# A decoder block on one core: the down projection's first 24 chunks by Strassen's seven products, and the second norm's factor moved to up's input

## The chip, the cores and the metric

The kernel runs on one core of a Trainium2 chip. TensorE multiplies matrices, VectorE (DVE in rows), ScalarE (ACT) and GpSimd (POOL) work elementwise, SyncE (SP) issues most transfers between memory and the on-chip buffers, and 16 DMA engines carry them out. The metric is the device time of one execution in microseconds; less is better.

## The reference

All tensors are float32; 512 tokens of width 1024.

```python
h = rms_norm(x, norm_mix)
q, k, v, u = split(h @ w_in)
a = moba_attention(q, k, v)                 # 8 heads x 64, causal, ALiBi
p = multiscale_pool(u, w_pool, pool_scale)  # 4 groups x 128
x = x + concat(a, p) @ w_out
h = rms_norm(x, norm_mlp)
x = x + square(relu(h @ w_up)) @ w_down     # w_up: 1024 x 4096, w_down: 4096 x 1024
out = rms_norm(x, norm_final)
```

## The kernel before

A float32 product is three matmuls (`mm3`): each operand is split into hi (the value rounded to float32r, a cast on ScalarE) and lo (the rest, a subtraction on VectorE), and hi x hi, hi x lo and lo x hi are summed in a bank of the accumulator. Every engine issues its instructions in the order in which the program is written (`in_program_order`), so an instruction that waits holds up all that stand behind it on its engine.

Weights come in chunks of 512 KB (128 partitions x 1024 numbers). `load` takes the next chunk from the list `chunks` and loads it into one of three buffers `raw` through SyncE's queue. `next_split` splits the oldest loaded chunk into `whi` and `wlo` (four buffers each) and calls `load` again; the load waits until the split has read its buffer. `prefetch` puts split chunks on the list `ready`.

The second half of the block is what matters here. `out_tile` adds the output projection to a tile of 128 tokens; `gained` multiplies the tile by the norm's weights, `turn2` transposes and splits it, and `factor` computes the second norm's factor of each row, which is not needed until the end: since it is positive, its square may be applied where the rows of the down projection are added to x (`residual`, with `rr`). Up takes 32 chunks of 128 hidden features; for each, 24 matmuls make a bank of 128 features x 512 tokens, and `sqrelu` writes the squared relu to `r[f]`. The down projection takes the 32 chunks of `w_down` in order. For chunk f, `r_split` splits `r[f]`, and 24 matmuls (4 token tiles x 2 halves of the columns x 3) add to all eight banks, which hold the sums of the whole stage. The last four chunks are held back and applied tile by tile, so that the residual, the final norm and the store of one tile run beside the products of the next.

## Time and profile before

| | |
|---|---|
| three runs | 546.05, 546.06 and 546.46 us, median 546.06 |
| the profiled execution | span 546.4 us from its first to its last instruction; no other time of its own is given |
| TensorE busy | 98% of the span |
| VectorE, ScalarE, GpSimd busy | 51%, 39%, 10% |
| memory read | 49.55 MB, 95 GB/s over the span with what is written |

The profile is of one execution. A matmul's busy time overlaps that of the next, so TensorE's pace is read from the starts of its instructions, not from their durations. Idle time of an engine is given with what released it. Where a helper writes an instruction, its line is the helper's: L112 is the cast and L113 the subtraction of every split, L161 to L163 are the three matmuls of `mm3`.

### The profile page before, as it was taken

To read this page: it belongs to the slowest core of one execution; us is meant where nothing else is said; L and a number is where in the kernel's file an instruction comes from. 1 tells how busy PE (TensorE), PEld (TensorE's weight loads), DVE (VectorE), ACT (ScalarE), POOL (GpSimd) and SP (SyncE) were. 2 spreads that over 40 slices of the span, in tenths; PEclk is the share of its full clock that TensorE was granted. 3 is DMA by queue.
4 is the path that set the end of the run, shared out by engine and by line. 5 is a ranking of instruction groups with operands and counts; after the bars stand their busy time and mean duration, and the time that the engine had idled before them with its cause. 6 is when DMAs were issued, how large, how long until landed. Compare 5 with 4: busy or idle time off the path is not lost.

```text
span 546.4 us, 6441 instructions
## 1 busy us (share of the span) xinstructions
PE 533.8 (98%) x2495; PEld 445.6 (82%) x2495; DVE 277.6 (51%) x468; ACT 215.4 (39%) x385; POOL 53.8 (10%) x55
## 2 busy tenths in 40 slices
...
GB/s 287 137 115 40 64 129 10 122 12 110 80 114 148 7 40 128 143 93 100 95 99 100 93 100 93 115 78 115 77 116 77 116 79 114 80 113 115 2 38 115
DMA packets 55904, 52.06 MB, mean 95 GB/s; under 512 B 2241, under 2 KB 47809, under 8 KB 55874
## 3 DMA queue, kind: packets, MB, share of 16 engines
...
q10 hardware_dynamic: 578, 1.05, 0.5%
...
HBM read 49.55 MB, written 2.10 MB: 95 GB/s over the span
## 4 chain that ended last, share of the span: by engine, by line
PE 89%; DVE 5%; ACT 2%; issue 2%; DMA 1%; SPq 0%; POOL 0%; POOLq 0%
PE bank L162 27%; PE bank L161 27%; PE bank L163 27%; PE bank L261 4%; PE bank L394 2%; DMA wvr<-in_w_in_dram 1%; PE bank L183 1%; PE bank L423 1%; DVE ptl L429 1%; DVE p L400 1%; DVE wlo L113 1%; DVE ka L366 1%; DVE mx L476 0%; PE bank L441 0%; DVE mx L475 0%
## 5 line engine op out<-in xcount | busy, mean ns | idle before, releaser
L161 PE MATMUL bank<-hh,whi 128*128 128x512 f32 (+1 forms) x376 | 141.7, 377 | 0.2 <-DVE qs L356 0.2
L163 PE MATMUL bank<-hh,wlo 128*128 128x512 f32 (+1 forms) x376 | 141.3, 376 | 0.0
L162 PE MATMUL bank<-hl,whi 128*128 128x512 f32 (+1 forms) x376 | 141.2, 376 | 0.0
L113 DVE TENSOR_TENSOR wlo<-raw,whi 128x1024 fp32r<-128x1024 f32 x73 | 90.4, 1242 | 97.6 <-ACT whi L112 97.3
L112 ACT CAST whi<-raw 128x1024 fp32r<-128x1024 f32 x76 | 79.5, 1055 | 92.7 <-PE bank L163 92.3
L161 PE MATMUL bank<-whi,rh 128*128 128x512 f32 x224 | 87.1, 389 | 0.0
L162 PE MATMUL bank<-wlo,rh 128*128 128x512 f32 x224 | 87.1, 389 | 0.0
L163 PE MATMUL bank<-whi,rl 128*128 128x512 f32 x224 | 87.1, 389 | 0.0
L161 PEld LDWEIGHTS bank<-hh,whi 128*128 128x128 f32 x376 | 70.8, 188 | 13.3 <-PE bank L423 0.4
L162 PEld LDWEIGHTS bank<-hl,whi 128*128 128x128 f32 x376 | 70.8, 188 | 12.8
L163 PEld LDWEIGHTS bank<-hh,wlo 128*128 128x128 f32 x376 | 70.8, 188 | 12.7
L630 DVE TENSOR_TENSOR r<-bank,z 128x512 f32<-128x512 f32 (+1 forms) x35 | 22.6, 645 | 97.2 <-ACT z L629 97.2
L629 ACT ACTIVATE z<-bank 128x512 f32<-128x512 f32 (+1 forms) x35 | 19.7, 562 | 118.1 <-PE bank L163 118.1
L161 PEld LDWEIGHTS bank<-whi,rh 128*128 128x128 f32 x224 | 42.1, 188 | 8.8
L163 PEld LDWEIGHTS bank<-whi,rl 128*128 128x128 f32 x224 | 42.1, 188 | 8.7
L162 PEld LDWEIGHTS bank<-wlo,rh 128*128 128x128 f32 x224 | 42.1, 188 | 8.6
L176 POOL TENSOR_TENSOR rstd<-ms,mhalf 128x1 f32<-128x1 f32 x8 | 4.4, 556 | 408.9 <-DVE ms L171 408.9
L113 DVE TENSOR_TENSOR rl<-r,rh 128x512 fp32r<-128x512 f32 x32 | 21.8, 684 | 4.7 <-ACT rh L112 4.7
L402 ACT ACTIVATE p<-p,mn 128x128 f32<-128x128 f32 (+3 forms) x32 | 18.0, 561 | 11.5 <-DVE rs L381 5.8
L112 ACT CAST rh<-r 128x512 fp32r<-128x512 f32 x32 | 19.8, 619 | 5.4 <-PE bank L162 5.4
L167 ACT ACTIVATE sq<-x 128x512 f32<-128x512 f32 (+2 forms) x17 | 10.3, 610 | 17.2 <-DVE x L658 17.2
L382 DVE TENSOR_SCALAR p<-p,rs 128x128 f32<-128x128 f32 (+3 forms) x32 | 16.0, 501 | 1.1
...
## 6 DMA issues: line engine op xcount, KB each, us to landing
raw<-in_w_up_dram SPq DMA_DIRECT2D x32, 512.0 KB, 4.0
raw<-in_w_down_dram SPq DMA_DIRECT2D x32, 512.0 KB, 3.3
raw<-in_w_in_dram SPq DMA_DIRECT2D x12, 512.0 KB, 4.1
raw<-in_w_out_dram SPq DMA_DIRECT2D x8, 512.0 KB, 3.3
wvr<-in_w_in_dram SPq DMA_DIRECT2D x4, 512.0 KB, 8.6
x<-in_x_dram SPq DMA_DIRECT2D x3, 512.0 KB, 9.7
out_dram<-o SPq DMA_DIRECT2D x4, 256.0 KB, 2.0
out_dram<-o ACTq DMA_DIRECT2D x4, 256.0 KB, 2.5
```

The source lines that it names most:

```text
L112: nc.scalar.copy(hi, src)
L113: (sub or nc.vector).tensor_sub(lo, src, as32(hi))
L161: nc.tensor.matmul(acc, lhsT=a[0], rhs=b[0], start=first, stop=False)
L162: nc.tensor.matmul(acc, lhsT=a[0], rhs=b[1], start=False, stop=False)
L163: nc.tensor.matmul(acc, lhsT=a[1], rhs=b[0], start=False, stop=last)
L167: nc.scalar.activation(dump, src, AF.Square, scale=1.0 / 32, accum_out=ss[:, k:k + 1])
L261: nc.tensor.matmul(acc, lhsT=a, rhs=w, start=n == 0 and kd == 0, stop=n == 2 and kd == KD - 1)
L382: nc.vector.tensor_scalar_mul(p[:, :w], p[:, :w], rs)
L394: nc.tensor.matmul(by_qi[qi], lhsT=qs[:, tok(qi)], rhs=k[:, :w], start=n == 0, stop=n == 1)
L402: nc.scalar.activation(p[:, :w], p[:, :w], AF.Exp, scale=-1.0, bias=mn, accum_out=sm)
L629: nc.scalar.activation(z[:, sl], acc, AF.Relu)
L630: nc.vector.tensor_mul(r[f][:, sl], acc, z[:, sl])
```

## The change

The first 24 chunks of the down projection are taken in 12 pairs. In a pair, the left operand is a 2 x 2 matrix of blocks (two chunks of features x two halves of the tokens) and so are the weights (two chunks x two halves of the columns). The four blocks of their product are made from seven products of sums of blocks in place of eight products. The eight banks can't hold seven products of two banks each, so there are two sweeps over the pairs: the first sums four products (m1, m6, m7, m4), whose banks are then read out into x and a helper tile y; the second sums three (m5, m2, m3). The sums of the token blocks are made on VectorE while up runs (`a_sums`, into `a_p`), and split once for each sweep (`a_split`). Of the four sums of weight blocks two are made on VectorE (`b_sums`) and two by a second DMA that GpSimd issues and that adds to what SyncE's load has put into the buffer (`accum_op`). Each chunk is loaded once for each sweep, whole or by half. A fourth `raw` buffer is added. The last eight chunks stay as they were, four as a plain loop and four tile by tile.

Because Strassen's sums mix token tiles, the second norm's factor can no longer be applied at the end: `normed2` applies it to up's input, after the squares (`squares`, `mean_of`, and `rsqrt`, a power on GpSimd); `gained`, `factor` and `rr` are gone, and `residual` is a plain addition.

```diff
 RAW = 3
+PAIRS = 12
...
     chunks += [cols_of(w_up_v, f * P) for f in range(NF)]
-    chunks += [rows_of(w_down, f) for f in range(NF)]
-    raws = []
+    for sweep in range(2):
+        for f in range(2 * PAIRS):
+            chunks.append(rows_of(w_down, f) + ((sweep, f % 2, f),))
+    chunks += [rows_of(w_down, f) for f in range(2 * PAIRS, NF)]
+    raws, more = [], []
     def load():
         if chunks:
-            src, shape = chunks.pop(0)
-            raw = wp.tile([P] + shape, F32, tag="raw", name="raw", bufs=RAW)
-            nc.sync.dma_start(raw, src)
+            src, shape, *pair = chunks.pop(0)
+            if more and len(more) % (RAW + 1) == 0:
+                raw = more[0].tile([P] + shape, F32, tag="raw", name="raw")
+            else:
+                raw = wp.tile([P] + shape, F32, tag="raw", name="raw", bufs=RAW)
+            if more:
+                more.append(None)
+            if not pair or pair[0][:2] == (1, 1):
+                nc.sync.dma_start(raw, src)
+            else:
+                sweep, half, f = pair[0]
+                if (sweep, half) == (0, 0):
+                    nc.sync.dma_start(raw[:, HALF[0]], src[:, HALF[0]])
+                elif (sweep, half) == (0, 1):
+                    nc.sync.dma_start(raw, src)
+                    above = w_down[0, (f - 1) * P:f * P, HALF[1]]
+                    nc.gpsimd.dma_start(raw[:, HALF[1]], above, accum_op=ALU.add)
+                else:
+                    nc.sync.dma_start(raw[:, HALF[1]], src[:, HALF[1]])
+                    nc.gpsimd.dma_start(raw[:, HALF[1]], src[:, HALF[0]], accum_op=ALU.add)
             raws.append((raw, shape))
...
-    rr = [const.tile([P, 1], F32, tag=f"rr{t}", name=f"rr{t}") for t in range(NT)]
-    def gained(t, half):
-        xg = pp.tile([P, T], F32, tag="p", name="xg", bufs=8)
-        nc.vector.tensor_mul(xg, x_t[t][:, HALF[half]], g_mlp[:, HALF[half]])
-        return xg
-    def factor(t):
-        ss = small.tile([P, 3], F32, tag="ss", name="ss")
-        for k, cols in enumerate(HALF):
-            squares(x_t[t][:, cols], pp.tile([P, T], F32, tag="p", name="sq", bufs=8), ss, k)
-        nc.vector.reciprocal(rr[t], mean_of(ss))
+    def normed2(t, rstd):
+        out = []
+        for cols in HALF:
+            xg = pp.tile([P, T], F32, tag="p", name="xg", bufs=8)
+            nc.vector.scalar_tensor_tensor(xg, x_t[t][:, cols], rstd, g_mlp[:, cols], op0=ALU.mult, op1=ALU.mult)
+            out.append(xg)
+        return out
...
     for t in range(NT):
-        xg = []
-        out_tile(t, range(4), wa, t == 0, lambda half: xg.append(gained(t, half)))
+        ss = small.tile([P, 3], F32, tag="ss", name="ss")
+        def done(half):
+            squares(x_t[t][:, HALF[half]], pp.tile([P, T], F32, tag="p", name="sq", bufs=8), ss, half)
+        out_tile(t, range(4), wa, t == 0, done)
+        rstd = rsqrt(mean_of(ss))
         if before is not None:
             turn2(t - 1, before)
-            factor(t - 1)
-        before = xg
+        before = normed2(t, rstd)
...
+    sp = ctx.enter_context(tc.tile_pool(name="sp", bufs=1, reuse_waits="tile"))
+    more += [sp] + [None] * RAW
+    load()
+    late = [sp.tile([P, T], F32, tag=f"r{f}", name=f"r{f}") for f in range(2 * PAIRS, NF)]
+    pairs = ExitStack()
+    ap = pairs.enter_context(tc.tile_pool(name="ap", bufs=1, reuse_waits="tile"))
+    HT = T // 2
+    a_p = [ap.tile([P, 7, HT], F32, tag=f"a{p}", name=f"a{p}") for p in range(PAIRS)]
+    def r_of(f):
+        if f >= 2 * PAIRS:
+            return late[f - 2 * PAIRS]
+        at_slot = 4 if f % 2 else 1
+        return a_p[f // 2][:, at_slot:at_slot + 2, :].rearrange("p s t -> p (s t)")
     def sqrelu(f, acc, sl=slice(None)):
-        z = mp.tile([P, T], F32, tag="z", name="z", bufs=2)
+        z = ap.tile([P, T], F32, tag="z", name="z")
         nc.scalar.activation(z[:, sl], acc, AF.Relu)
-        nc.vector.tensor_mul(r[f][:, sl], acc, z[:, sl])
-    def r_split(f):
-        r_s = [mp.tile([P, T], F32R, tag=f"r{k}", name=f"r{k}", bufs=LAST + 1) for k in "hl"]
-        split_into(*r_s, r[f])
-        return r_s
+        nc.vector.tensor_mul(r_of(f)[:, sl], acc, z[:, sl])
+    def a_sums(p):
+        a = a_p[p]
+        nc.vector.tensor_sub(a[:, 6, :], a[:, 1, :], a[:, 2, :])
+        nc.vector.tensor_sub(a[:, 2, :], a[:, 5, :], a[:, 2, :])
+        nc.vector.tensor_add(a[:, 0, :], a[:, 1, :], a[:, 2, :])
+        nc.vector.tensor_sub(a[:, 3, :], a[:, 4, :], a[:, 0, :])
+    def a_split(p, sweep):
+        src = a_p[p][:, 2:5, :]
+        if sweep == 0:
+            src = a_p[p].rearrange("p s t -> p (s t)")
+            src = bass.AP(tensor=src.tensor, offset=src.offset, ap=[src.ap[0], [5 * HT, 2], [1, 2 * HT]])
+        n = 4 - sweep
+        hi, lo = [sp.tile([P, 4, HT], F32R, tag=f"a{k}", name=f"a{k}", bufs=2) for k in "hl"]
+        if sweep == 0:
+            views = [v.rearrange("p (i j) t -> p i (j t)", j=2) for v in (hi, lo)]
+        else:
+            views = [v[:, :n, :] for v in (hi, lo)]
+        split_into(*views, src)
+        return hi, lo
+    def b_sums(sweep):
+        (r0, _), (r1, _) = raws[:2]
+        if sweep == 0:
+            nc.vector.tensor_add(r0[:, HALF[1]], r1[:, HALF[1]], r0[:, HALF[0]])
+            nc.vector.tensor_add(r1[:, HALF[0]], r1[:, HALF[0]], r0[:, HALF[1]])
+    def b_split(cols=slice(None)):
+        raw, shape = raws.pop(0)
+        hi = wp.tile([P] + shape, F32R, tag="whi", name="whi")
+        lo = wp.tile([P] + shape, F32R, tag="wlo", name="wlo")
+        split_into(hi[:, cols], lo[:, cols], raw[:, cols])
+        load()
+        ready.append((hi, lo))
+    steps = [(sweep, half) for sweep in range(2) for p in range(PAIRS) for half in range(2)]
+    steps += [(2, 0)] * (2 * (NF // 2 - PAIRS) - LAST)
+    def advance():
+        if not steps:
+            return
+        sweep, half = steps.pop(0)
+        if half == 0 and sweep < 2:
+            b_sums(sweep)
+        b_split(HALF[1] if (sweep, half) == (1, 0) else slice(None))
+    a_s = []
     for f in range(NF):
         if f < HALVED:
             up(first[f][1][:, :T // 2], w_first[f], slice(T // 2, T))
...
             acc = bank()
             up(acc, ready.pop(0))
             sqrelu(f, acc)
-        prefetch(1)
+        if f < NF - 4:
+            prefetch(1)
+        else:
+            advance()
         if f == 4:
             g_fin = bcast_row(norm_final)
-        if f == NF - 3:
-            rs = [r_split(0)]
-    accs = [[bank() for _ in range(2)] for _ in range(NT)]
+        if f % 2 and f < 2 * PAIRS:
+            a_sums(f // 2)
+        if f == NF - 2:
+            a_s.append(a_split(0, 0))
+    banks = [[bank() for _ in range(2)] for _ in range(4)]
+    m1, m6, m7, m4 = banks
+    def half_of(k):
+        return slice(k * P, (k + 1) * P)
+    def product(accs, a, s, w, cols, first, last):
+        for j in range(2):
+            mm3(accs[j], (a[0][:, s, half_of(j)], a[1][:, s, half_of(j)]), (w[0][:, cols], w[1][:, cols]), first, last)
+    for p in range(PAIRS):
+        a, first, last = a_s.pop(0), p == 0, p == PAIRS - 1
+        a_s.append(a_split(p + 1, 0) if not last else a_split(0, 1))
+        w = ready.pop(0)
+        product(m1, a, 1, w, HALF[0], first, last)
+        product(m6, a, 0, w, HALF[1], first, last)
+        advance()
+        w = ready.pop(0)
+        product(m7, a, 3, w, HALF[1], first, last)
+        product(m4, a, 2, w, HALF[0], first, last)
+        if not last:
+            advance()
+    def x_at(i, j, cols):
+        return x_t[2 * i + j][:, HALF[cols]]
+    y = hp.tile([P, 4, T], F32, tag="hh", name="y")
+    for j in range(2):
+        nc.scalar.copy(y[:, j, :], m1[j])
+    for j in range(2):
+        nc.vector.tensor_add(x_at(0, j, 0), m1[j], x_at(0, j, 0))
+    for j in range(2):
+        nc.vector.tensor_sub(y[:, j, :], m6[j], y[:, j, :])
+    for j in range(2):
+        nc.vector.tensor_sub(y[:, 2 + j, :], y[:, j, :], m7[j])
+    advance()
+    for j in range(2):
+        nc.vector.tensor_add(x_at(1, j, 0), m4[j], x_at(1, j, 0))
+    for j in range(2):
+        nc.vector.tensor_add(x_at(0, j, 1), x_at(0, j, 1), y[:, j, :])
+        nc.vector.tensor_sub(x_at(1, j, 0), x_at(1, j, 0), y[:, 2 + j, :])
+        nc.vector.tensor_add(x_at(1, j, 1), x_at(1, j, 1), y[:, 2 + j, :])
+    m5, m2, m3 = m1, m6, m7
+    for p in range(PAIRS):
+        a, first, last = a_s.pop(0), p == 0, p == PAIRS - 1
+        if not last:
+            a_s.append(a_split(p + 1, 1))
+        else:
+            pairs.close()
+            mp = ctx.enter_context(tc.tile_pool(name="mp", bufs=1, reuse_waits="tile"))
+            def r_split(f):
+                r_s = [mp.tile([P, T], F32R, tag=f"r{k}", name=f"r{k}", bufs=LAST + 1) for k in "hl"]
+                split_into(*r_s, late[f - 2 * PAIRS])
+                return r_s
+            rs = [r_split(2 * PAIRS)]
+        w0, w1 = ready.pop(0), ready.pop(0)
+        product(m5, a, 0, w0, HALF[1], first, last)
+        product(m2, a, 2, w1, HALF[0], first, False)
+        product(m3, a, 1, w1, HALF[1], first, False)
+        advance()
+        advance()
+    for i in range(2):
+        for j in range(2):
+            nc.vector.tensor_sub(x_at(i, j, 1), x_at(i, j, 1), m5[j])
+    accs = [[m2[0], m3[0]], [m2[1], m3[1]], [m5[0], m4[0]], [m5[1], m4[1]]]
...
     def residual(acc, t, cols):
-        nc.vector.scalar_tensor_tensor(x_t[t][:, cols], acc, rr[t], x_t[t][:, cols], op0=ALU.mult, op1=ALU.add)
+        nc.vector.tensor_add(x_t[t][:, cols], acc, x_t[t][:, cols])
...
-    for f in range(NF - LAST):
+    for f in range(2 * PAIRS, NF - LAST):
         w, r_s = ready.pop(0), rs.pop(0)
         rs.append(r_split(f + 1))
         for t in range(NT):
             for k, cols in enumerate(HALF):
-                down(accs[t][k], r_s, w, t, cols, f == 0, f == NF - LAST - 1 and (t, k) == (NT - 1, 1))
-        if f + 5 <= NF - LAST:
-            prefetch(1)
+                down(accs[t][k], r_s, w, t, cols, f == 2 * PAIRS and t >= 2,
+                     f == NF - LAST - 1 and (t, k) == (NT - 1, 1))
+        if steps:
+            advance()
```

VectorE, the middle of the down projection. Names are the program's tiles with numbers: before, `wlo` is the low part of a chunk's weights (made of `raw` and `whi`) and `rl` that of a chunk's features (line 113). Two chunks of the kernel before are:

```order
L113 TENSOR_TENSOR wlo_3700<-raw_3601,whi_3699 128x1024
L113 TENSOR_TENSOR rl_3706<-r14_2133,rh_3705 128x512
L113 TENSOR_TENSOR wlo_3734<-raw_3635,whi_3733 128x1024
L113 TENSOR_TENSOR rl_3740<-r15_2134,rh_3739 128x512
L113 TENSOR_TENSOR wlo_3768<-raw_3669,whi_3767 128x1024
L113 TENSOR_TENSOR rl_3774<-r16_2135,rh_3773 128x512
```

In the changed kernel's first sweep, two pairs (four chunks) are the following rows, where line 137 is the split, lines 698 and 699 are the sums of weight blocks, and `al` is the low part of a pair's four token operands:

```order
L698 TENSOR_TENSOR raw_3259<-raw_3297,raw_3259 128x512
L699 TENSOR_TENSOR raw_3297<-raw_3297,raw_3259 128x512
L137 TENSOR_TENSOR wlo_3370<-raw_3259,whi_3369 128x1024
L137 TENSOR_TENSOR wlo_3388<-raw_3297,whi_3387 128x1024
L137 TENSOR_TENSOR al_3395<-a3_2135,ah_3394 128x1024
L698 TENSOR_TENSOR raw_3330<-raw_3348,raw_3330 128x512
L699 TENSOR_TENSOR raw_3348<-raw_3348,raw_3330 128x512
L137 TENSOR_TENSOR wlo_3413<-raw_3330,whi_3412 128x1024
L137 TENSOR_TENSOR wlo_3431<-raw_3348,whi_3430 128x1024
L137 TENSOR_TENSOR al_3438<-a4_2136,ah_3437 128x1024
```

Two sums have come in ahead of each pair's splits; the first of them reads both buffers of the pair, so it stands behind the odd chunk's load and its accumulation, and all the splits stand behind it.

VectorE, between the sweeps of the changed kernel (nothing stood here before; the kernel before has one sweep). Lines 774 to 785 read the banks into x and `y` and add `y` to x:

```order
L778 TENSOR_TENSOR y_3814<-y_3814,bank_3305 128x512
L137 TENSOR_TENSOR wlo_3824<-raw_3736,whi_3823 128x1024
L781 TENSOR_TENSOR x2_75<-bank_3306,x2_75 128x512
L781 TENSOR_TENSOR x3_76<-bank_3307,x3_76 128x512
L783 TENSOR_TENSOR x0_73<-x0_73,y_3814 128x512
L784 TENSOR_TENSOR x2_75<-x2_75,y_3814 128x512
L785 TENSOR_TENSOR x2_75<-x2_75,y_3814 128x512
L783 TENSOR_TENSOR x1_74<-x1_74,y_3814 128x512
L784 TENSOR_TENSOR x3_76<-x3_76,y_3814 128x512
L785 TENSOR_TENSOR x3_76<-x3_76,y_3814 128x512
L137 TENSOR_TENSOR al_3838<-a1_2133,ah_3837 128x768
```

The token operand of the second sweep's second pair, `al_3838`, stands last in this row, behind all reading of banks and all additions.

GpSimd, its last stretch. Before, after the last of the mixer's work (line 450), it had the powers of the final norm (line 176) and the last tile's products:

```order
L450 TENSOR_TENSOR cl_121<-cl_121,fix 64x512 x2
L176 TENSOR_TENSOR rstd<-ms,mhalf 128x1 x3
L697 TENSOR_TENSOR o<-x_76,grow 128x512
L697 TENSOR_TENSOR o<-x_76,grow 128x320
L699 TENSOR_TENSOR ss<-ss 128x1
```

Now the same place reads as follows, with the mixer's line 474, the power in line 200, and the accumulating DMAs in lines 129 and 132:

```order
L474 TENSOR_TENSOR cl_121<-cl_121,fix 64x512 x2
L200 TENSOR_TENSOR rstd<-ms,mhalf 128x1 x4
L129 DMA raw<-in_w_down_dram 128x512 x12
L132 DMA raw<-in_w_down_dram 128x512 x12
L200 TENSOR_TENSOR rstd<-ms,mhalf 128x1 x3
L857 TENSOR_TENSOR o<-x_76,grow 128x512
```

Four powers (the second norm's) and 24 DMAs have come in; the DMAs stand in one row and have GpSimd to themselves.

## Rows read from the trace of the kernel before

**Rows 1.** The page, parts 1 and 4: busy shares, and the chain that ended last.

```profile
PE 533.8 (98%) x2495; PEld 445.6 (82%) x2495; DVE 277.6 (51%) x468; ACT 215.4 (39%) x385; POOL 53.8 (10%) x55
...
PE 89%; DVE 5%; ACT 2%; issue 2%; DMA 1%; SPq 0%; POOL 0%; POOLq 0%
```

**Rows 2.** Window of the down projection: us, busy (count) PE, PEld, DVE, ACT, POOL, clock, DMA, GB/s.

```profile
365.00:515.00 150.00, 150.00 (x664) 124.24 (x663) 54.79 (x61) 47.14 (x61) 0.00 (x0) 1.00 0.28 94
```

**Rows 3.** ScalarE in order of time, down projection: start, duration, operation, [idle before].

```profile
382.12 1.05 ACT L112 CAST whi<-raw 128x1024 fp32r<-128x1024 f32 x1 [3.87 <-PE bank L163]
...
387.56 1.05 ACT L112 CAST whi<-raw 128x1024 fp32r<-128x1024 f32 x1 [3.87 <-PE bank L163]
```

**Rows 4.** VectorE in order of time, where its operations stand back to back.

```profile
499.19 1.22 DVE L113 TENSOR_TENSOR wl_l<-raw,wl_h 128x1024 fp32r<-128x1024 f32 x1
500.33 0.68 DVE L113 TENSOR_TENSOR rl<-r,rh 128x512 fp32r<-128x512 f32 x1
500.93 1.22 DVE L113 TENSOR_TENSOR wl_l<-raw,wl_h 128x1024 fp32r<-128x1024 f32 x1
```

**Rows 5.** Groups of instructions, 365 to 515 us: busy us, mean ns, idle before.

```profile
L113 DVE TENSOR_TENSOR wlo<-raw,whi 128x1024 fp32r<-128x1024 f32 x25 | 30.6, 1225 | 86.5 <-ACT whi L112 86.5
...
L113 DVE TENSOR_TENSOR rl<-r,rh 128x512 fp32r<-128x512 f32 x31 | 21.1, 684 | 4.7 <-ACT rh L112 4.7
L112 ACT CAST rh<-r 128x512 fp32r<-128x512 f32 x31 | 19.2, 619 | 5.4 <-PE bank L162 5.4
```

**Rows 6.** DMA issues: queue, count, KB each, median us from issue to landing.

```profile
raw<-in_w_down_dram SPq DMA_DIRECT2D x32, 512.0 KB, 3.3
...
x<-in_x_dram SPq DMA_DIRECT2D x3, 512.0 KB, 9.7
out_dram<-o SPq DMA_DIRECT2D x4, 256.0 KB, 2.0
...
x<-in_x_dram SPq DMA_DIRECT2D x2, 256.0 KB, 3.2
```

**Rows 7.** DMA view of the first 15 us, 40 slices: GB/s moved.

```profile
GB/s 0 0 0 0 76 229 388 311 339 219 120 137 147 115 218 273 284 344 350 311 339 393 377 377 404 399 404 421 399 415 415 432 426 410 393 418 392 380 326 335
```

**Rows 8.** TensorE in order of time, 130 to 134 us: start, duration, [idle before].

```profile
130.71 0.50 PE L161 MATMUL bank<-mxh,wplh 128*128 128x512 f32 x1 [1.51 <-ACT wplh L112]
...
132.52 0.47 PE L394 MATMUL bank<-ka,qs 128*128 128x128 f32 x1 [0.55 <-DVE ka L366]
133.67 0.45 PE L394 MATMUL bank<-kb,qs 128*128 128x128 f32 x1 [0.68 <-DVE kb L370]
```

**Rows 9.** The window behind them, columns as in rows 2.

```profile
133.60:138.50 4.90, 4.83 (x16) 4.47 (x17) 4.20 (x12) 4.65 (x9) 0.90 (x1) 0.50 0.01 3
```

**Rows 10.** The last token tile and its norm, engine by engine in order of time.

```profile
188.57 0.40 PE L163 MATMUL bank<-wah,cl 128*128 128x512 f32 x1
...
195.43 1.04 PE L183 MATMUL bank<-ident,xg 128*128 128x128 f32 x8
...
189.01 0.69 DVE L507 TENSOR_TENSOR x<-bank,x 128x512 f32<-128x512 f32 x1 [1.31 <-PE bank L163]
...
191.03 0.63 ACT L167 ACTIVATE sq<-x 128x512 f32<-128x512 f32 x1
191.55 0.20 ACT L167 ACTIVATION_READ_ACCUMULATOR sq<-x 128x1 f32 x1
```

**Rows 11.** Groups of instructions over the span: the powers and the scalings by them.

```profile
L176 POOL TENSOR_TENSOR rstd<-ms,mhalf 128x1 f32<-128x1 f32 x8 | 4.4, 556 | 408.9 <-DVE ms L171 408.9
...
L244 DVE SCALAR_TENSOR_TENSOR xn<-x,rstd,bank 128x512 f32<-128x512 f32 x8 | 5.8, 744 | 2.8 <-POOL rstd L176 2.8
```

**Rows 12.** GpSimd and VectorE in order of time, at 125 us.

```profile
125.06 4.72 POOL L113 TENSOR_TENSOR wlo<-raw,whi 128x1024 fp32r<-128x1024 f32 x2
125.06 2.42 DVE L475 TENSOR_TENSOR mx<-us,rc 128x16 f32<-128x16 f32 x1
```

**Rows 13.** All instances of line 475: least, median and longest ns.

```profile
L475 DVE TENSOR_TENSOR mx<-us,rc x4: 167/168/2421, 66.3 to 125.1; 128x16 f32<-128x16 f32 x4
```

3 lines of the change are left out of this document (removed).

## The prediction

> **What bounds the kernel now.** I read the page's shares and its chain first: TensorE is busy for 98% of the span and the chain that ended last lies on it for 89% [rows 1]. Then the stage that the change rewrites, the down projection, as one window (365 to 515 us): TensorE is busy in all 150 us at the full clock, VectorE in 55 of them, ScalarE in 47, GpSimd in none, and the DMA engines carry a share of 0.28 [rows 2]. The order of time on ScalarE shows the beat: one cast of a weight chunk every 5.44 us [rows 3], set by TensorE, since a chunk is 24 matmuls of 512 columns: 5.44 / 24 = 0.2267 us each. So a matmul left out here is worth 0.2267 us, as long as what feeds TensorE keeps the new beat. The reader should see how much room the feeders have: of a beat VectorE needs 1.14 + 0.60 us, which are its start-to-start times for 1024 and 512 columns [rows 4]; ScalarE casts for 1.05 and 0.62 us [rows 5].
>
> **What the change removes.** Two chunks (a pair) cost 48 matmuls; by the seven products it is 24 in the first sweep and 18 in the second: 6 fewer, in 12 pairs. 72 x 0.2267 = **-16.3 us**. A pair's beat becomes 5.44 us in sweep one and 4.08 us in sweep two, where it was 10.88 in all.
>
> **What feeds sweep one.** Per pair VectorE now does two sums of 512 columns and three differences of 1024: 2 x 0.60 + 3 x 1.14 = 4.62 us. With the wait of the first difference for its cast (which waits for the first sum) it is 0.69 + 1.05 + 3 x 1.14 + hand-offs of 0.04, about 5.25 of 5.44: it fits, with 0.2 us over. ScalarE (3 casts, 3.2 us) fits.
>
> The tight part is the ring of four raw buffers, which is two pairs long. Follow the buffer of an odd chunk: accumulation landed, first sum 0.69, cast 1.05, difference of the even chunk 1.14, its own difference 1.23, four hand-offs of 0.04: 4.3 us. Then SyncE's load of 512 KB, 3.3 us from issue to landing [rows 6], less 0.1 that the smaller neighbour gives back. Then GpSimd's accumulating DMA, A us. The turn takes 7.5 + A and must fit in two beats, 10.88: no wait while A is at most 3.4. In sweep two the even chunk's turn is a cast of 0.62, a difference of 0.68, a load of 256 KB (between 2.0 and 3.2 us by rows of that size; I take 2.6) and A: 4.1 + A in 8.16 us, free up to 4.1.
>
> The trace has no accumulating DMA and none that GpSimd issues. From below, A is the shortest row of 256 KB, a store with 2.0 us [rows 6]; from above it is a load in a queue full of others, 9.7 us [rows 6]. Between them I take the row whose bytes are nearest: an accumulation reads 256 KB from memory, reads as much in the tile and writes it back, so it is near to the 512-KB load of the same weights, **A = 3.3 us**. The Trainium skill speaks against a lower value: "Collectives: The Full Stack", section on the bandwidth ceiling in Part 3, says that a reducing DMA is slowed not by the addition but by its two source reads, on one read ring, so that it delivers half of a copy's rate. No run here shows it yet. By that page 256 KB cost as 512 KB do; by bytes alone A would be some 2.6 us and this term 3 us smaller.
>
> With 3.3 the turn is 10.8 of 10.88 us, no spare. While an accumulation moves, the loads of the other pair share the engines; per pair 1 MB is loaded, against 1 MB per 10.88 us before, whose share was 0.28 [rows 2], so their share is 0.56, and the accumulations come on top. The engines can carry it (over 400 GB/s where loads queued, [rows 7]; 1 MB in 5.44 us is 193), but it lengthens single transfers. I put 0.6 us on a turn of sweep one: about five turns run, **+3 us**. It is 0 if A is 2.0, and it has no bound that matters above (the rival below).
>
> **The change of sweeps.** Call T the end of sweep one on TensorE. VectorE issues in program order: the difference of half a chunk, whose buffer TensorE frees at T - 2.7, ends near T - 1.2 (0.62 + 0.68 and hand-offs). Then six operations that read banks (at 0.60 to 0.69, to T + 2.5), a whole chunk's difference (T + 3.6), two more bank reads (T + 4.9), six additions in x (T + 8.5), and only then the difference of the token operand of sweep two's second pair (768 columns, between the rows of 512 and 1024: 0.96), T + 9.5. TensorE finishes the first pair at T + 4.08 and needs that operand in its third matmul, at T + 4.5. It waits **5.0 us**. The first pair's own banks are read just before they are wanted. From below 3.5, if the reads of banks start earlier than I think; from above 7, if VectorE comes late from sweep one.
>
> **The clock.** In the old trace TensorE stood idle before 130.71, 132.52 and 133.67 us in short pieces (1.51 us the longest), and then ran 4.9 us at a granted clock of 0.50, its lower level of 1.2 GHz [rows 8, 9]. Work in that time takes twice as long, so it gave up 2.4 us. A single wait of 5 us should do the same: **+2.4 us**, 0 if the clock stays.
>
> **The eight late chunks.** The last turn of sweep two casts a chunk whose buffer is freed at its end T2: cast and difference end at T2 + 2.6, then four subtractions of m5. The third of them frees the bank of the third token tile at T2 + 4.5; TensorE has 12 matmuls, 2.7 us, ahead of that tile. **+1.8 us** (0 to 2.4).
>
> **The second norm's factor.** Now up's input waits for squares, the mean, GpSimd's power of 0.56 us and two scalings of 0.74 [rows 11]. From a tile's last product (188.57 for the last) it is: addition 0.69, square 0.63 + 0.20, mean 0.17 (as the small sum of [rows 13]), power 0.56, the other tile's casts and differences that lie between on the same engines, two scalings 1.49, about 5.2 us in all. TensorE turns that tile's blocks 6.2 us later (24 matmuls and eight transposes), and for the last tile at 195.43, after two half-chunks of up [rows 10]. Hidden, **0**; without that cover it would be up to 5 us.
>
> **Also hidden.** The sums of token blocks in up (four of 256 columns every second chunk, below 2.4 us by the row of 512, in 10.88 us of which VectorE uses 2 x (1.23 + 0.69)) and one buffer for z instead of two.
>
> **Sum.** -16.3 + 3 + 5.0 + 2.4 + 1.8 = -4.1. The profiled execution spans 546.4 us, and there is nothing around it that the times show: the median of the runs is 546.06, 0.3 below. So 542.3 in a profile and **542 us** as a median.
>
> **Rivals.**
> *The accumulation is slow, and the ring of weights becomes the bound* (slower than before). Every microsecond of A above 3.4 adds 0.5 us to each pair of sweep one, and above 4.1 to each of sweep two. For A = 5: 0.8 x 10 pairs, 6 for sharing, 0.45 x 11: 19 us in place of my 3, so 558. It decides from A = 4, where stalls of 7 us eat the rest of the gain. For it: GpSimd's issue comes after the load's landing, nothing in this trace shows how long it takes, and loads in company took 9.7 us [rows 6]. Against it: single loads here land in 3.3 us.
>
> *The transfers hide altogether* (A of 2.6 or less): 542 - 3 = 539; 536.5 if the clock also stays up. For it: the 256-KB store at 2.0 us.
>
> *GpSimd's issuing holds VectorE up.* In this trace a sum of 16 columns took 2.42 us instead of 0.17, beside a GpSimd operation on SBUF [rows 12, 13]. If each of the 12 issues of sweep one held VectorE for 1 us, its 5.25 would be 6.25 of 5.44, some 10 us more in all: 551. The Trainium skill ("SBUF — State Buffer", section Who interferes with whom) says that a VectorE operation with two SBUF inputs is blocked by a GpSimd instruction that reads SBUF, not by one that only writes there, as the writing of descriptors would be. By that rule this rival falls; the row above agrees with the rule's first half and doesn't show the second.
>
> **How the numbers follow.** My case (A of 2.8 to 3.9) gives 538 to 546: chance 0.42. Transfers hidden, 534 to 539: 0.17. The slow ring, 546 to 580: 0.36. GpSimd against VectorE, 550 to 560: 0.05. The range that leaves out less than 2 in 10 is 534 to 561, since it cuts only the far end of the slow ring. A measurement here tells 0.2% (1.1 us) from no change: faster 0.56, same 0.08 (the edge of my case and of the slow ring), slower 0.36.
>
> **What would show it.** In the profile after: matmuls of the sweeps 0.227 apart; a landing time of some 3.3 us behind the accumulating issues; gaps on TensorE of 1 us or less in sweep one, one gap of about 5 us between the first and second pair of sweep two, released by VectorE's difference of the token operand, with a granted clock of 0.50 behind it; a gap of 2 us three tiles' worth into the late chunks. Gaps of 2 us and more at every second pair of sweep one, ended by a sum that waited for a DMA, would prove me wrong to the slow side; a span under 538 to the other.

## The result, and the profile after

The changed kernel takes 569.5 us (median of four runs, 569.26 to 569.59) against 546.3 for the kernel before on the same chip: ratio 1.0415, 95% interval 1.040 to 1.0431. Slower by 4%, where 542 was forecast; the time lies above the range.

The profiled execution spans 567.7 us, 21.3 more than the 546.4 of before (the medians differ by 23.2, since the profiled execution of before is a longer one than its median: see the end). The page's busy times, and the shares of its chain:

```profile
PE 532.1 (94%) x2423; PEld 437.2 (77%) x2423; DVE 353.2 (62%) x578; ACT 242.1 (43%) x411; POOL 77.2 (14%) x83
...
DMA 13%; PE 11%; DVE 6%; issue 3%; ACT 2%; POOL 0%; POOLq 0%; ACTq 0%; DVEq 0%
```

TensorE does 72 matmuls less, as it should (2423, 2495 before), and yet ends later. The chain's shares can't be set beside the 89% TensorE of before [rows 1], for it could be followed back only to 366.8 us (they sum to 35% here, to 99% there). In what it covers, the two sweeps and the end, DMAs from `w_down` into `raw` come first, 13% of the span or 74 us, ahead of TensorE's 11%. Windows over the two sweeps (columns as in [rows 2]: us, TensorE, weight loads, VectorE, ScalarE, GpSimd, clock, DMA share, GB/s) show where:

```profile
365.01:381.30 16.29, 16.29 (x73) 13.52 (x72) 12.17 (x14) 8.40 (x9) 1.76 (x2) 1.00 0.48 126
381.30:437.00 55.70, 46.84 (x179) 35.77 (x178) 34.60 (x36) 20.61 (x21) 7.02 (x8) 0.91 0.57 151
437.00:452.20 15.20, 9.37 (x39) 6.79 (x37) 8.79 (x11) 7.10 (x10) 1.75 (x2) 1.00 0.55 142
452.20:467.40 15.20, 11.80 (x36) 9.08 (x37) 13.00 (x19) 4.33 (x6) 1.76 (x2) 0.78 0.46 134
467.40:484.00 16.60, 16.60 (x75) 13.71 (x73) 9.74 (x11) 8.81 (x11) 2.65 (x3) 1.00 0.76 187
484.00:511.60 27.60, 23.48 (x90) 17.43 (x89) 15.55 (x17) 12.46 (x16) 3.53 (x4) 0.94 0.79 217
```

Three pairs of sweep one run at the full pace (first window). From then on TensorE stands idle in both sweeps, except for a few pairs in the middle of sweep two; VectorE is busy for 34.6 of 55.7 us in the second window; it has least room at the change of sweeps (13.0 of 15.2 in the fourth). TensorE in order of time, the first product of sweep one, the longer waits, and the first product of the eight late chunks (start, duration, [idle before, what ended it]):

```profile
365.01 0.39 PE L185 MATMUL bank<-whi,ah 128*128 128x512 f32 x1
...
395.39 0.50 PE L185 MATMUL bank<-whi,ah 128*128 128x512 f32 x1 [2.48 <-ACT ah L136]
...
425.81 0.79 PE L185 MATMUL bank<-whi,ah 128*128 128x512 f32 x1 [3.22 <-ACT ah L136]
...
452.25 0.50 PE L185 MATMUL bank<-whi,ah 128*128 128x512 f32 x1 [4.26 <-DVE x L774]
...
462.04 0.50 PE L187 MATMUL bank<-whi,al 128*128 128x512 f32 x1 [3.35 <-DVE al L137]
...
515.70 0.39 PE L185 MATMUL bank<-whi,rh 128*128 128x512 f32 x1
...
520.07 0.50 PE L185 MATMUL bank<-whi,rh 128*128 128x512 f32 x1 [1.48 <-DVE x L810]
```

From the first row to that of 515.70 are 504 matmuls, which at 0.2267 us make 114.2 us; they took 150.7. I call the difference, 36.5, the **excess**. From the starts of its pairs it falls into these parts: pairs 4 to 11 of sweep one 16.2; the change of sweeps (the last pair of sweep one and the first two of sweep two, with the low clock behind their waits) 12.8; the other pairs of sweep two 7.5; the first three pairs none. Before, the same 24 chunks took 130.6 us without any excess. So 36.45 - 16.32 = 20.1, plus 1.8 in the late chunks and the tail (52.0 against 50.2), less 0.6 by which the first product starts earlier: the 21.3.

**The ring.** What the wait of 395.39 goes back to is in order on VectorE and ScalarE: the first sum of weight blocks waits for a DMA into `raw`, the casts wait for the sum, and the token operand's cast, for which TensorE waits, stands behind them.

```profile
391.54 0.69 DVE L698 TENSOR_TENSOR raw<-raw 128x512 f32<-128x512 f32 x1 [3.98 <-DMA raw<-in_w_down_dram]
...
394.29 1.04 ACT L136 CAST ah<-a 128x1024 fp32r<-128x1024 f32 x1
```

This is the kind of gap that the prediction named as the sign of its slow side; two of them (395.39 and 425.81) are over 2 us. One turn of an odd chunk's buffer, in the middle of sweep one: SyncE's load, GpSimd's adding DMA, VectorE's sum and splits, the next load into it. The rows are in order of time, from several engines:

```profile
400.42 0.89 POOL L129 DMA_DIRECT2D raw<-in_w_down_dram  x1 [7.22 <-DVE wlo L137]
401.21 0.33 SPq L127 DMA_DIRECT2D raw<-in_w_down_dram  x1
407.08 0.69 DVE L699 TENSOR_TENSOR raw<-raw 128x512 f32<-128x512 f32 x1
407.20 0.88 POOL L129 DMA_DIRECT2D raw<-in_w_down_dram  x1 [5.90 <-DVE raw L698]
410.57 1.22 DVE L137 TENSOR_TENSOR al<-a,ah 128x1024 fp32r<-128x1024 f32 x1
411.71 0.68 DVE L698 TENSOR_TENSOR raw<-raw 128x512 f32<-128x512 f32 x1
...
416.04 0.33 SPq L127 DMA_DIRECT2D raw<-in_w_down_dram  x1
```

and from issue to landing, for the adding DMA of 400.42 (it belongs to the other pair in the ring), the load of 401.21 and the adding DMA of 407.20:

```profile
DMA to landing us min/median/max: 5.9/5.9/5.9
...
DMA to landing us min/median/max: 5.3/5.3/5.3
...
DMA to landing us min/median/max: 3.7/3.7/3.7
```

So the load, issued at 401.21, landed at 406.5, in 5.3 us where single loads before took 3.3 [rows 6], since the even chunk's load of 256 KB had gone out 1.14 us ahead of it and the other pair's adding DMA was moving at the same time and took 5.9 itself. GpSimd issued the buffer's own addition 0.7 us after this landing (the page puts the wait down to VectorE's sum; in the program the instruction waits for the landing, and 0.55 to 0.75 us lie behind every landing, also where VectorE stood idle). It took 3.7 us, alone. Then the sum came 0.8 us late, behind `al` of the pair ahead. Sums, casts and splits took 4.3, as reckoned. The turn is 14.8 us in place of 10.8, and two beats are 10.88. The other pair's buffer turned as slowly (its load went out at 395.86, the next one at 410.69): there the load met no addition and landed after 3.9 us, but the addition, that of 400.42, took the 5.9. So each turn meets the other pair's transfers once. While they met, the 16 engines had a mean share of 0.81 (columns as above):

```profile
401.20:406.00 4.80, 4.80 (x22) 3.97 (x21) 1.12 (x1) 0.00 (x0) 0.11 (x1) 0.98 0.81 221
```

The page's rows on queues and issues (packets, MB, share of the 16 engines' span; count, KB, median us to landing):

```profile
q0 software_dynamic: 3456, 6.29, 6.9%
...
raw<-in_w_down_dram SPq DMA_DIRECT2D x32, 512.0 KB, 4.2
raw<-in_w_down_dram SPq DMA_DIRECT2D x24, 256.0 KB, 2.8
raw<-in_w_down_dram POOLq DMA_DIRECT2D x24, 256.0 KB, 4.2
```

GpSimd's queue holds only the 24 adding DMAs: 6.9% of 567.7 us is 39.2, so 1.63 us of all 16 engines for each 256 KB.

### The profile page after: what moved, and what is told of

Same layout as the page of the kernel before. It is cut to its first block, busy times and chain, and to the rows that moved or that the text cites. A ratio compares the mean times of both kernels' runs of the same rounds, so it can differ in the third digit from the quotient of the medians.

```text
span 567.7 us, 6603 instructions
## 1 busy us (share of the span) xinstructions
PE 532.1 (94%) x2423; PEld 437.2 (77%) x2423; DVE 353.2 (62%) x578; ACT 242.1 (43%) x411; POOL 77.2 (14%) x83
## 3 DMA queue, kind: packets, MB, share of 16 engines
q0 software_dynamic: 3456, 6.29, 6.9%
## 5 line engine op out<-in xcount | busy, mean ns | idle before, releaser
L137 DVE TENSOR_TENSOR wlo<-raw,whi 128x1024 fp32r<-128x1024 f32 x97 | 112.3, 1170 | 45.3 <-ACT whi L136 44.8
L136 ACT CAST whi<-raw 128x1024 fp32r<-128x1024 f32 (+1 forms) x100 | 97.7, 1000 | 89.3 <-DVE raw L698 39.8
L185 PE MATMUL bank<-whi,ah 128*128 128x512 f32 x168 | 70.1, 417 | 14.0 <-ACT ah L136 9.7
L187 PE MATMUL bank<-whi,al 128*128 128x512 f32 x168 | 70.2, 418 | 8.2 <-DVE al L137 8.1
L186 PE MATMUL bank<-wlo,ah 128*128 128x512 f32 x168 | 69.0, 411 | 0.0
L185 PEld LDWEIGHTS bank<-whi,ah 128*128 128x128 f32 x168 | 33.6, 200 | 23.7 <-ACT ah L136 12.3
L187 PEld LDWEIGHTS bank<-whi,al 128*128 128x128 f32 x168 | 33.6, 200 | 20.0 <-DVE al L137 13.0
L186 PEld LDWEIGHTS bank<-wlo,ah 128*128 128x128 f32 x168 | 33.9, 202 | 7.3
L137 DVE TENSOR_TENSOR al<-a,ah 128x1024 fp32r<-128x1024 f32 (+1 forms) x24 | 26.0, 1085 | 0.0
L136 ACT CAST ah<-a 128x1024 fp32r<-128x1024 f32 (+1 forms) x24 | 22.5, 938 | 0.0
```

Of the source, the lines that this page charges most:

```text
L136: nc.scalar.copy(hi, src)
L137: (sub or nc.vector).tensor_sub(lo, src, as32(hi))
L185: nc.tensor.matmul(acc, lhsT=a[0], rhs=b[0], start=first, stop=False)
L186: nc.tensor.matmul(acc, lhsT=a[0], rhs=b[1], start=False, stop=False)
L187: nc.tensor.matmul(acc, lhsT=a[1], rhs=b[0], start=False, stop=last)
```

## The experiments

Theory R: the ring of raw buffers turns too slowly, because of the adding DMAs. Theory V: VectorE's longer list is the bound. Theory P: GpSimd's part (its issues, or its use of the on-chip memory) is. For every kernel the excess is taken as above, from its own trace; the first product of sweep one starts between 362.6 and 365.4 us in these kernels, although nothing ahead of it was touched but a buffer or two, so spans alone are less sharp than the excess. Every kernel of the table but the first and the last ran once, and the kernel before took 545.6 to 548.4 us in its runs beside them: a difference of 2 or 3 us between two times says little by itself. "Edges" are the change of sweeps and the start of the late chunks.

| kernel | span | first product, late chunks | excess |
|---|---|---|---|
| the changed kernel | 567.7 | 365.01, 515.70 | 36.5 |
| no second DMA | 537.4 | 363.79, 485.50 | 7.5 |
| plain second DMA | 551.2 | 364.25, 499.26 | 20.8 |
| half the addition | 554.4 | 363.63, 502.47 | 24.6 |
| sums on VectorE | 548.5 | 365.37, 496.58 | 17.0 |
| one of these sums on GpSimd | 550.5 | 364.35, 498.64 | 20.0 |
| banks read first | 563.6 | 362.60, 511.67 | 34.8 |
| fifth raw buffer | 549.2 | 363.64, 497.17 | 19.3 |
| fifth raw buffer, edges mended | 542.6 | 363.68, 492.36 | 14.4 |
| sums on VectorE, edges mended | 543.4 | 363.05, 493.25 | 16.0 |
| the same, interleaved | 529.8 | 363.29, 479.69 | 2.2 |

**Without the second DMA.**

```diff
                     nc.sync.dma_start(raw, src)
-                    above = w_down[0, (f - 1) * P:f * P, HALF[1]]
-                    nc.gpsimd.dma_start(raw[:, HALF[1]], above, accum_op=ALU.add)
...
                     nc.sync.dma_start(raw[:, HALF[1]], src[:, HALF[1]])
-                    nc.gpsimd.dma_start(raw[:, HALF[1]], src[:, HALF[0]], accum_op=ALU.add)
```

> The changed kernel without its second, adding DMAs (so two of the four sums of weight blocks are left out; everything else stays). Theory R, the ring of raw buffers turns too slowly because of the adding DMAs: the excess of the middle pairs of sweep one (16.2 us) and of the later pairs of sweep two (7.5 us) goes, and with it most of the wait at the reading of the banks (6.0 with its clock); the wait for the second pair's token operand stays (5.3 with its clock): 538 us, 535 to 543. Rival V, VectorE's longer list is the bound (5.25 of 5.44 us, with the wait for the cast more): sweep one keeps beats of 5.8 us and more, over 550. Rival P, GpSimd's writing of descriptors slows VectorE: as R here, but the beats would have shown longer VectorE operations in the changed kernel.

Measured 539.2 us (547.9 for the kernel before beside it), span 537.4. Windows of sweep one, of the change of sweeps, and of the rest of sweep two:

```profile
363.79:429.07 65.28, 65.28 (x289) 54.07 (x288) 56.26 (x61) 36.89 (x39) 0.00 (x0) 1.00 0.45 146
429.07:438.30 9.23, 4.70 (x21) 3.57 (x19) 9.23 (x16) 4.08 (x5) 0.00 (x0) 0.93 0.28 85
438.30:444.00 5.70, 5.65 (x14) 4.45 (x15) 3.30 (x4) 0.62 (x1) 0.00 (x0) 0.51 0.51 167
444.00:485.50 41.50, 41.50 (x185) 34.36 (x183) 27.60 (x30) 23.73 (x30) 0.00 (x0) 1.00 0.60 194
```

TensorE has no gap in the 65.28 us of sweep one, which is 288 x 0.2267: every pair takes 5.44 us with VectorE's list unchanged. So V falls for the changed kernel. P falls by the changed kernel's own rows: VectorE's sum beside GpSimd's issue (407.08 and 407.20 above) took its 0.69 us, and so did the others that met an issue. R stands: all of the excess but 7.5 us at the change of sweeps hangs on the second DMA, 30 us of the span in all. The loads of odd chunks show what the even chunk's load alone does to them, since here no addition moves; their shortest, median and longest time to landing from 371.5 to 411 us, 1.1 to 1.2 us behind the even one's load:

```profile
DMA to landing us min/median/max: 3.6/3.8/4.3
```

The change of sweeps is the one place left, and it is the wait of the prediction, on TensorE and at VectorE's row for the token operand:

```profile
438.35 0.80 PE L184 MATMUL bank<-whi,al 128*128 128x512 f32 x1 [4.59 <-DVE al L134]
```

with a clock of 0.51, the lower level, in the 5.7 us behind it (third window): 4.6 of wait, 2.7 of clock.

**What of the second DMA costs: the addition, its bytes, or its queue.** Two kernels on this. One writes the same bytes without adding:

```diff
-                    nc.gpsimd.dma_start(raw[:, HALF[1]], above, accum_op=ALU.add)
+                    nc.gpsimd.dma_start(raw[:, HALF[1]], above)
...
-                    nc.gpsimd.dma_start(raw[:, HALF[1]], src[:, HALF[0]], accum_op=ALU.add)
+                    nc.gpsimd.dma_start(raw[:, HALF[1]], src[:, HALF[0]])
```

> The second DMA on GpSimd's queue stays, with its bytes, its wait for the load's landing and its place, but it overwrites in place of adding (the two sums are left out). If the addition's reading of the tile is what costs (its packets hold the 16 engines 1.63 us for 256 KB where a load of 256 KB holds them 0.83): landing 2.9 us alone in place of 3.7 and 4.5 in place of 6 beside a load, a turn of the ring of 12.3 in place of 14.8, about 10 us less in all: 557 (552 to 561). If the queue's fixed cost and the wait for the landing are what costs: landing stays within 0.3 of 3.7 and the time above 564.

The other adds half as much:

```diff
-                    nc.gpsimd.dma_start(raw[:, HALF[1]], above, accum_op=ALU.add)
+                    nc.gpsimd.dma_start(raw[:, 512:768], above[:, :256], accum_op=ALU.add)
...
-                    nc.gpsimd.dma_start(raw[:, HALF[1]], src[:, HALF[0]], accum_op=ALU.add)
+                    nc.gpsimd.dma_start(raw[:, 512:768], src[:, 0:256], accum_op=ALU.add)
```

> The changed kernel with half of each addition: the adding DMAs carry 256 columns (128 KB) in place of 512, the other half of those two sums is left out. If an addition costs by its bytes, at twice a copy's: landing some 2.9 us alone and 4.5 beside a load, as the plain copies of 256 KB had, and a span within 3 us of theirs (551.2): 549 to 554. If it has a large fixed cost that a copy has not: landing stays above 3.4 alone and the span above 559.

Plain: 553.0 us, span 551.2. Its queue, and the shortest, median and longest time to landing of its 24 second DMAs:

```profile
q0 software_dynamic: 1920, 6.29, 3.5%
...
DMA to landing us min/median/max: 2.8/3.0/5.1
```

Half: 556.5 us, span 554.4:

```profile
q0 software_dynamic: 3456, 3.15, 3.9%
...
DMA to landing us min/median/max: 3.1/3.7/5.7
```

The plain copy holds the engines 3.5% of 551.2 / 24 = 0.80 us for 256 KB, half of the addition's 1.63; half the addition, with as many packets as the whole (3456), holds them 0.90. So the engines' time goes nearly by bytes, twice over for an addition. The plain copy came out as its first expectation had it (landing 2.8 alone and 3.5 to 4.5 in sweep one beside a load; 553.0 in 552 to 561). The Trainium skill's rule that the prediction took for its 3.3 ("Collectives: The Full Stack", section on the bandwidth ceiling in Part 3) agrees with these rows: half of a copy's rate. To landing, unhindered, it is 3.6 (256 KB added), 3.1 (128 KB) and 2.8 (256 KB copied), so my 2.9 for the half addition missed by 0.2, the span by 0.4, and the longest landing, 5.7, lies over the 4.5 that I expected beside a load; the alternative of a large fixed cost (over 3.4, over 559) is further off. Of the 30 us the addition makes 16.5, and a mere second copy in GpSimd's queue, with its pick-up and its company, 13.8.

**Length of the turn, or throughput.** A fifth raw buffer; to make room, the relu writes into the features' buffer:

```diff
-            if more and len(more) % (RAW + 1) == 0:
-                raw = more[0].tile([P] + shape, F32, tag="raw", name="raw")
+            if more and len(more) % (RAW + 2) < 2:
+                raw = more[0].tile([P] + shape, F32, tag="raw", name="raw", bufs=2)
...
-    more += [sp] + [None] * RAW
-    load()
+    more += [sp] + [None] * (RAW + 1)
+    for _ in range(2):
+        load()
...
-        z = ap.tile([P, T], F32, tag="z", name="z")
+        z = r_of(f)
         nc.scalar.activation(z[:, sl], acc, AF.Relu)
-        nc.vector.tensor_mul(r_of(f)[:, sl], acc, z[:, sl])
+        nc.vector.tensor_mul(z[:, sl], acc, z[:, sl])
```

> The changed kernel with its adding DMAs and a fifth raw buffer (the room comes from the relu, which now writes into the features' own buffer in place of a helper tile). If the turn's length is what costs: a turn of 14.8 us lies over 2.5 beats in place of 2, 5.9 us a pair in place of 7.4, and in sweep two the turn fits; some 12 + 6 us less and part of the wait at the reading of the banks: 547 us, 542 to 553. If the DMA engines' throughput is what costs, a deeper ring gives nothing: 564 or more, with the same landing times.

551.0 us, span 549.2, with all 24 adding DMAs in place. Their median to landing is even longer, 4.9 us in place of 4.2, and the engines carry more per microsecond (DMA share 0.83 in sweep two, 0.76 to 0.79 before):

```profile
363.64:436.00 72.36, 66.72 (x289) 53.46 (x287) 54.49 (x57) 34.34 (x36) 10.54 (x12) 1.00 0.67 173
...
450.00:497.17 47.17, 43.92 (x189) 34.72 (x188) 28.78 (x32) 23.71 (x30) 6.18 (x7) 1.00 0.83 233
```

So it was the length of the turn against the ring's depth; the engines could carry more. One buffer of 512 KB gives back 17 us. The time lies in the range of the first expectation, in its upper half: the longer landings leave 19.3 us of excess, half of it at the change of sweeps.

**The change of sweeps by itself.** The banks of m1 and m6 are read as soon as they are done, ahead of the next split, and the eight other additions go into sweep two one by one (`next(later, ...)` issues the next of them):

```diff
         product(m6, a, 0, w, HALF[1], first, last)
+        if last:
+            for j in range(2):
+                nc.scalar.copy(y[:, j, :], m1[j])
+            for j in range(2):
+                nc.vector.tensor_add(x_at(0, j, 0), m1[j], x_at(0, j, 0))
+            for j in range(2):
+                nc.vector.tensor_sub(y[:, j, :], m6[j], y[:, j, :])
         advance()
...
             a_s.append(a_split(p + 1, 1))
+            if first:
+                advance()
+            else:
+                next(later, lambda: None)()
```

> The changed kernel with its adding DMAs, but the banks of m1 and m6 are read before the next split of weights is issued, and the eight other additions at the change of sweeps are spread over sweep two, one a pair, so that the token operand's difference no longer stands behind them. Theory: the two waits at the change (4.26 and 3.35 us) and the low clock behind them (1.7 each) come from VectorE's order, so up to 11 us go, less some 2 because the ring is then the next to be late: 558 us, 555 to 562. Rival: they are the ring's lateness in another place, and move into the next pairs: 565 or more.

565.4 us: the expectation of 558 was wrong, its rival right. The first three pairs of sweep two now run at 4.08 us, but the wait shows up in the pairs on both sides (9.1 and 9.6 us for the last two of sweep one, up to 6.8 for the last of sweep two); the excess falls by 1.6 alone. While the ring is late, mending another wait moves it on. With the deeper ring the same edit, with m5's subtractions moved ahead of the last splits, should count:

```diff
         product(m3, a, 1, w1, HALF[1], first, False)
+        if last:
+            for i in range(2):
+                for j in range(2):
+                    nc.vector.tensor_sub(x_at(i, j, 1), x_at(i, j, 1), m5[j])
         advance()
         advance()
-    for i in range(2):
-        for j in range(2):
-            nc.vector.tensor_sub(x_at(i, j, 1), x_at(i, j, 1), m5[j])
```

> Adding DMAs kept, with the fifth raw buffer, and the edges mended: banks of m1 and m6 read before the next split, the eight other additions spread over sweep two, m5's four subtractions ahead of the last splits. If the deeper ring has left the change of sweeps a matter of VectorE's order, its 4.0 and 2.3 us of waits, 2.8 of low clock and the 1.5 at the late chunks go: 549.2 - 10 = 539 in the profile (536 to 542). If the ring is still late there, the waits move on, as they did with four buffers: 546 or more.

544.3 us, span 542.6: 6.6 less, not 10. The waits at the change and at the late chunks are gone, but pairs 6, 8, 9 and 12 of sweep one and six pairs of sweep two still wait for the ring. It lies between the two expectations.

**The sums on VectorE in place of the adding DMAs.** SyncE loads whole chunks:

```diff
+            nc.sync.dma_start(raw, src)
...
-        if sweep == 0:
+        if sweep == 1:
+            nc.vector.tensor_add(r0[:, HALF[1]], r0[:, HALF[1]], r0[:, HALF[0]])
+        else:
+            nc.vector.tensor_add(r1[:, HALF[1]], r1[:, HALF[1]], r0[:, HALF[1]])
             nc.vector.tensor_add(r0[:, HALF[1]], r1[:, HALF[1]], r0[:, HALF[0]])
```

> All four sums of weight blocks on VectorE, whole chunks loaded by SyncE, no adding DMA; the whole computation is done. R: VectorE needs 3 x 0.60 + 3 x 1.14 and a wait of 0.5 for the cast, 5.75 of 5.44 us, so sweep one loses up to 0.3 us a pair in its later half, about 2; the rest as without the second DMA: 541 us, 538 to 546. V: VectorE as the bound loses the 0.3 on top of the changed kernel's excess: over 565.

550.3 us, 19 less than the changed kernel, but 4 over what I expected at most. VectorE in a pair of sweep one:

```profile
404.62 1.22 DVE L124 TENSOR_TENSOR al<-a,ah 128x1024 fp32r<-128x1024 f32 x1
405.76 0.69 DVE L687 TENSOR_TENSOR raw<-raw 128x512 f32<-128x512 f32 x1
406.48 0.69 DVE L688 TENSOR_TENSOR raw<-raw 128x512 f32<-128x512 f32 x1
407.21 0.69 DVE L689 TENSOR_TENSOR raw<-raw 128x512 f32<-128x512 f32 x1
408.42 2.36 DVE L124 TENSOR_TENSOR wlo<-raw,whi 128x1024 fp32r<-128x1024 f32 x2 [0.52 <-ACT whi L123]
```

A sum that reads what the one ahead of it wrote starts 0.72 us after it, not 0.60 as independent operations do [rows 4], and with the wait for the cast the list takes 6.07 us of 5.44. Here V holds: from the seventh pair on the pairs take 6.07 us, in sweep two 4.47 of 4.08. And the change of sweeps costs 10.8 us of excess with no ring late.

**One of these sums on GpSimd.**

```diff
-            nc.vector.tensor_add(r1[:, HALF[1]], r1[:, HALF[1]], r0[:, HALF[1]])
+            nc.gpsimd.tensor_add(r1[:, HALF[1]], r1[:, HALF[1]], r0[:, HALF[1]])
```

> As the kernel with all four sums on VectorE, but the first sum of each pair of sweep one on GpSimd (the whole computation is done). If GpSimd's operation runs beside VectorE's: VectorE is back at 5.3 us a pair, the beats of 6.07 go, 550.3 - 4 = 546 (544 to 548). If it blocks VectorE's operations with two operands (the third rival of the prediction, by the row of 2.42 us): VectorE's rows beside it are longer than 0.69 and 1.22 us, and the time is 551 or more.

552.5 us: it blocks. GpSimd's sum, and VectorE's two differences beside it, which took 2.36 above:

```profile
409.80 1.89 POOL L687 TENSOR_TENSOR raw<-raw 128x512 f32<-128x512 f32 x1 [4.56 <-DMA raw<-in_w_down_dram]
...
409.31 3.46 DVE L124 TENSOR_TENSOR wlo<-raw,whi 128x1024 fp32r<-128x1024 f32 x2 [0.52 <-ACT whi L123]
```

VectorE loses 1.1 us to save 0.72, and the pairs take 6.44.

**All four sums on VectorE, with the edges mended**, by the two diffs on the change of sweeps and on m5:

> All four sums on VectorE, the banks of m1 and m6 read before the next split, the eight other additions spread over sweep two, and the four subtractions of m5 ahead of the last two splits of the sweep. Here no ring is late, so the waits at the change of sweeps (2.05 and 7.95 us of excess in the kernel with sums on VectorE) and that at the late chunks (1.5) should go: 11 less; but VectorE is the bound in both sweeps (6.07 and 4.47 us a pair) and gets 0.6 more in eight pairs of sweep two, about 5 back: 544 us, 540 to 547. If those waits come from the ring, nothing goes: 550 or more.

545.4 us (span 543.4), as expected: 5 us less than without. m5's wait at the late chunks is gone, the first pairs of sweep two lose 2 us in place of 8; VectorE, now with 0.6 more in eight pairs, makes pairs of 5.07 us.

**The same, with VectorE's order changed** so that the token operand's difference fills the wait for the cast:

```diff
+        b_sums(sweep, 0)
         a_s.append(a_split(p + 1, 0) if not last else a_split(0, 1))
+        b_sums(sweep, 1)
...
+                if steps[0][0] < 2:
+                    b_sums(1, 0)
+                a_s.append(a_split(p + 1, 1))
+                next(later, lambda: None)()
```

Here the first part of `b_sums` makes two of sweep one's three sums, or sweep two's single one, and the second part the third sum.

> As the last one, and VectorE's order is changed so that it waits for no cast: in sweep one the first two sums, the token operand's difference, the third sum, the two differences of weights (0.72 + 0.60 + 1.14 + 0.60 + 2 x 1.14 = 5.34 us of 5.44), in sweep two sum, token operand, an addition, the differences (3.82 of 4.08). Theory: then nothing but the 72 matmuls is left, 546.1 - 16.3 and up to 3 us for waits at the edges: 531 us, 529 to 535. Rival: two whole loads a pair make the ring late without any addition (4.3 us to landing): 538 or more.

532.9 us against 546.8 for the kernel before on the same chip: ratio 0.9749, interval 0.9725 to 0.9774, faster than both kernels. The profiled run spans 529.8. VectorE in a pair of sweep one, and the windows of the two sweeps:

```profile
405.03 0.69 DVE L691 TENSOR_TENSOR raw<-raw 128x512 f32<-128x512 f32 x1
405.75 0.69 DVE L692 TENSOR_TENSOR raw<-raw 128x512 f32<-128x512 f32 x1
406.36 1.22 DVE L124 TENSOR_TENSOR al<-a,ah 128x1024 fp32r<-128x1024 f32 x1
407.50 0.69 DVE L686 TENSOR_TENSOR raw<-raw 128x512 f32<-128x512 f32 x1
408.10 2.56 DVE L124 TENSOR_TENSOR wlo<-raw,whi 128x1024 fp32r<-128x1024 f32 x2
410.58 0.69 DVE L691 TENSOR_TENSOR raw<-raw 128x512 f32<-128x512 f32 x1
```

```profile
363.29:430.00 66.71, 66.39 (x293) 54.47 (x292) 63.90 (x73) 37.78 (x40) 0.00 (x0) 1.00 0.59 190
430.00:479.69 49.69, 48.56 (x215) 39.85 (x213) 45.75 (x59) 28.45 (x36) 0.00 (x0) 1.00 0.79 245
```

TensorE works through both windows but for 1.4 us. VectorE's list is 5.55 us a pair, a little over the beat, which the two pairs split ahead carry to the end of the sweep. Two whole loads a pair are no trouble (4.0 us to landing in the median): the rival on the ring falls.

**The second norm alone**, in the kernel before: `normed2` and `rsqrt` as in the diff ahead, the down projection as it was, a plain addition at the end.

> The kernel before with the second norm's factor on up's input alone (squares, mean, power on GpSimd, two scalings for each tile; a plain addition at the end) and the down projection as it was. The prediction has it hidden behind 24 matmuls and eight transposes of the tile before: no difference, 546.1 within 1.1 us. If the chain of 5.2 us stood open at the last tile or the first, up to 5 us more: 549 to 551.

Ratio 1.0001, interval 0.9987 to 1.0014; in its trace TensorE has no idle time from 180 us to the end. It costs nothing.

## Why the prediction was wrong, step by step

- **72 matmuls, -16.3 us: right.** Without the second DMA the pairs take 5.44 and 4.08 us exactly.
- **The ring, +3 us: this step failed.** It measured 16.2 us in sweep one and 7.5 in sweep two, for which nothing was put, and it lengthened the change of sweeps by 5.3 (below). The prediction had the right place, the turn of an odd chunk's buffer, and the right room, 10.88 us; it put the turn at 7.5 + A = 10.8 with A = 3.3 and 0.6 for sharing. Measured 14.8: load 5.3 in place of 3.2, pick-up by GpSimd 0.7, for which the sum had no term, A 3.7 in place of 3.3, and 0.8 behind VectorE's token operand, which the sum of single durations did not have. The largest part is the sharing: 2.1 us on a turn, where I took 0.6. Some 0.6 of the 2.1 is the even chunk's load, 1.14 us ahead (3.8 us to landing without any second DMA, 3.8 to 3.9 in the changed kernel where no addition moved), which the prediction had give back 0.1; the other 1.5 is the other pair's addition. In the other pair's turn it is the addition that pays: A is 5.9. The sharing was sized by the DMA share of a window (0.28 for 1 MB in 10.88 us, so 0.56), but a mean share says nothing of transfers that start 0.5 to 0.9 us apart in every turn. The turn itself times them so: a buffer's load goes out when the other pair's addition does. The row that hinted at it stood in [rows 6]: loads in company took 9.7 us. In sweep two it is the same: the even buffer loaded at 475.52 turned in 11.1 us where 8.16 were to be had, with a load of 5.1 in place of 2.6, 0.7 of pick-up, A of 3.9, and 1.5 of cast, difference and hand-offs.
- **The slow ring as a rival: right.** Its stretch of 546 to 580 holds the result, and the sign named for it came. What it was to hang on is only half of the matter: it was to decide from A = 4, and alone A is 3.6 to 3.9, below that point. It moved A and left the load and the pick-up as they were; what decides is the turn in company, and counted as that shows it, 14.8 - 7.5, A is 7.3.
- **The change of sweeps, 5.0 + 2.4 us: right in its own kernel, wrong in this one.** Without the second DMA it is 4.6 of wait and 2.7 to 2.9 of clock and edges, 7.5 in all, and the token operand's difference ends at T + 9.2, where T + 9.5 was reckoned (T is 429.07 there). In the changed kernel it is 12.8, because "the first pair's own banks are read just before they are wanted" fell: the split ahead of these reads in VectorE's order waited for an addition to land, so m1's banks were read from 451.5 on, and TensorE stood 4.26 us before the second sweep's first product; 3.35 us of the other wait followed.
- **The clock: right.** 0.51 behind the wait without the second DMA; in the changed kernel also at 397, 427 and 506 us, 1.7 to 2.3 us each, inside the ring's sums above.
- **The late chunks, +1.8: right** (52.0 against 50.2 us; the wait of 1.48 at 520.07 is the bank of m5). Moving four subtractions ahead of two splits took it away.
- **The second norm, 0: right** by the run of it alone.
- **GpSimd against VectorE: did not come.** VectorE's sums beside the issues of adding DMAs keep their 0.69 us (407.08). GpSimd's own arithmetic does block, as the run shows. The page that was named for this, "SBUF — State Buffer" of the Trainium skill, agrees in both halves now.

Why a transfer in company takes 5.3 to 6.5 us is shown in part. By the shares of the queues, the even load, the odd load and the addition would hold the 16 engines some 0.8, 1.6 and 1.6 us, 4.0 together (an estimate); from 401.2 to 406.0, up to 0.5 us before the last of them landed, the engines were busy for 0.81 x 4.8 = 3.9 us. So each landing has in it most of the engines' time of all three. What stays open is why the addition and the odd load land together, 0.2 us apart. The Trainium skill ("DMA: Bandwidth & Descriptors", section SWDGE vs HWDGE vs iDMA) says that an engine goes round between its queues; that both land late together agrees with it, but no run here took the two apart. Open too is why the first product of sweep one starts at times up to 2.8 us apart.
